# A four-layer fp32 trunk on one core: raw input transposed, its norm moved onto products, and a later order of heads

## The chip, the cores and the metric

The kernel runs on one core of one Trainium2 chip. What counts is the device time of one execution in microseconds (us). The engines are named as the profile names them: PE is TensorE (PEld its weight loads), DVE VectorE, ACT ScalarE, POOL GpSimd, SP SyncE, whose queue issues most DMAs. Each engine runs its own instructions strictly in program order.

## What is computed

A trunk of 256 tokens by 2048 channels with two mixers: a gated DeltaNet, an MLP, a sparse attention (DSA), an MLP, a final norm. The change touches the first mixer alone, apart from arguments.

```python
def rms_norm(x, g):
    y = xf * lax.rsqrt(jnp.mean(xf * xf, axis=-1, keepdims=True) + EPS)
    return y * g

def gated_deltanet(h, w_in, conv_w, a_log, dt_bias, out_norm, w_out):
    proj = h @ w_in                                  # h = rms_norm(x, norm_mix[0]); q, k, v, z, b, a
    qkv = silu(causal_conv(qkv, conv_w))             # 16 q/k heads, 32 v heads of 128
    q, k = l2norm(q) * 128 ** -0.5, l2norm(k)
    beta, g = sigmoid(b), -exp(a_log) * softplus(a + dt_bias)
    o = chunk_gated_delta_rule(q, k, v, g, beta)     # a triangular inverse in each chunk
    o = rms_norm(o, out_norm) * silu(z)
    return o @ w_out
...
h = h + gated_deltanet(rms_norm(h, norm_mix[0]), ...)
h = h + squared_relu_mlp(rms_norm(h, norm_mlp[0]), mlp_w_up[0], mlp_w_down[0])
```

## The kernel before

Every large product is made of three passes in a rounded fp32 format: each weight item of 128x1024 numbers is loaded as `raw`, copied by ACT to `whi`, and its rest made by DVE as `wlo` (class `Stream`, lines 131 to 173). `get` (line 144) hands out one item and keeps three items split ahead and four more loading. `mm3` (line 321) issues hi*hi, hi*lo and lo*hi. `by_channel` (line 359) and `by_token` (line 377) run such a product over their items. This is the **main stream** of PE; 24 of its matmuls with 256 columns, or 12 with 512, use up one item.

The opening (lines 402 to 470) loads `x` into `xin` in four quarters on the SP queue, then `ident` and eight rows of gains, squares `x`, makes the reciprocal root, scales `xin` in place (`normalise`) and transposes it block by block into `xT` (`first`). Weights are asked for behind those loads on the same queue.

The first mixer runs 16 groups `g` (lines 736 to 752), each with a `by_channel` of eight items for one q/k head and two v heads, an evacuation of its two PSUM banks into `s`, and a `by_token` of four items for the gate `z`. Small work runs beside it in generators: `delta(g)` (line 520) does the convolution and the masked products of one group; every second one goes on into `solved(p)` (line 598), which inverts the triangles of a pair of groups in four levels of 32x32 matmuls, joins them, applies them, normalises the result `o` (tile `Tt`) and transposes it into `hT`. Pair p holds heads 4p to 4p+3. Then the out-projection (line 758) takes its four column chunks: three of them early, without the last heads, then their late rest, then the fourth.

What sets the order is a planner at build time. `Pace` (line 28) keeps a modelled clock for each engine; after each k `bg.tick()` lets those generators advance whose modelled time has come. `ensure(key)` (line 345) is the other way in: where the main stream needs a result that isn't emitted yet, it calls `bg.step()` until it is, and each such step advances the **oldest** active generator (line 109), whichever one holds the key. What is emitted in this way stands on PE with no main matmul in between. The keys are `("v", g - 2)` before the evacuation of group g (line 739), since `s` has two buffers, and `("o", k)` for head k in the out-projection (line 388).

```python
    def ensure(key):
        while key not in ready:
            assert bg.step(), key
...
        chain = self.active[0] if due is None else min(self.active, key=lambda c: c[0])
```

In the rows of the order and the trace, `aux`, `acc` and `pk` are PSUM tiles; `aux<-Tc,yv` (after the change `aux<-Tc,Lc`) and `aux<-Lc,Tct` (`aux<-Pm,Tct`) are the two halves of a level, `aux<-r,Tt`, `aux<-yv,la` and `aux<-Tt,yv` the application of the inverse, `aux<-wide,Tt` the transposes of `o` by `ident`, `aux<-wide,s` those of v, and `acc<-xhi,whi`, `acc<-whi,xhi`, `acc<-whi,h` and their like the main stream.

Of the kernel before, what the change touches and what calls it, by code (L numbers as in the profile page):

```python
# [7 lines left out]
F32 = mybir.dt.float32  # L8
F32R = mybir.dt.float32r
I32 = mybir.dt.int32  # L10
AF = mybir.ActivationFunctionType
# [119 lines left out]
class Stream:  # L131
# [11 lines left out]

    def get(self):
# [3 lines left out]
        while self.split < min(i + ahead + 1, len(self.items)) or self.loaded < min(i + self.loads + 1, len(self.items)):  # L148
            while self.loaded < min(self.split + self.loads - self.ahead, len(self.items)):
                (n, w), pieces, _ = self.items[self.loaded]  # L150
                raw = self.raw_pool.tile([P, 1024], F32, name="raw")
                view = raw[:, : n * w].rearrange("p (n w) -> p n w", n=n)
                for at, src in pieces:
                    self.sync.dma_start(out=at(view), in_=src)
                self.raw[self.loaded] = raw
                self.loaded += 1
# [20 lines left out]
def tile_hybrid_trunk(ctx: ExitStack, tc: tile.TileContext, a: dict, out: bass.AP):  # L177
# [103 lines left out]
    add_mix_out(s_o, 16, 2)  # L281
# [114 lines left out]
    def early_chunks(tiles, key, nk, banks=()):  # L396

        outs = [by_token(nk // 2 - 2, h_part(tiles), key, outs=o) for o in (None, None, *banks)]
        return [by_token(2, h_part(tiles), key, outs=o, k0=nk - 4) for o in outs]


    with tc.tile_pool(name="first", bufs=1) as fp:
        xin = fp.tile([P, 2, D], F32, name="xin")
        rows = fp.tile([P, P], F32, name="rows")
# [5 lines left out]
        dve.memset(rows, 0.0)  # L410
        at = 0
        VEC = {}
        for name, src in (
# [7 lines left out]
        pool.dma_start(out=cwr, in_=a["dn_conv_w"][0].rearrange("t (c p) -> (t c) p", p=P).rearrange("(n q) p -> q n p", q=P))  # L421
# [694 lines left out]
```

## Time and profile before

| | us |
|---|---|
| median of three runs (lowest, highest) | 2590.46 (2588.62, 2592.14) |
| the profiled execution | 2591.25 |
| its span, first to last instruction | 2589.2 |
| PE busy in the span | 2545.4 |
| first matmul of the main stream | 18.28 |
| last group of the first mixer ends at about | 742 |

The engine with the most work is PE. A row of the timeline has its start, its duration, engine, operation, tiles (out<-in) and, in brackets, the idle time of the engine before it with what ended that. The idle time of an engine other than PE is of no concern by itself. All times below are of the profiled execution, from the start of its span.

### The profile page before, as it was taken

How to read it: one execution, taken by the hardware profiler on the slowest of the kernel's cores; microseconds unless marked ns; L12 is line 12 of the kernel's file. 1: busy time of each engine (PE TensorE's matmuls, PEld its weight loads, DVE VectorE, ACT ScalarE, POOL GpSimd, SP SyncE). 2: the span in 40 equal slices, each digit the busy share in tenths (PEclk: the TensorE clock that was granted, in tenths of full speed). 3: DMA queues.
4: the chain of work that ended last, by engine and by line, in shares of the span. 5: the costliest groups of instructions: out<-in, count | busy, mean ns of one | idle time of the engine just before them, and what ended most of it. 6: DMA issues, size and time to landing. Idle time of an engine off the chain costs nothing.

```text
span 2589.2 us, 52473 instructions
## 1 busy us (share of the span) xinstructions
PE 2545.4 (98%) x21827; PEld 2331.0 (90%) x21827; DVE 1534.8 (59%) x2179; ACT 1272.8 (49%) x1890; POOL 302.3 (12%) x512
## 2 busy tenths in 40 slices
PE   7999999999999999999999999999999999999998
PEld 7999999999977799988899988898899988999886
DVE  5867677668764655554455555576555544555544
ACT  5555555655544444443344444566544433444443
POOL 0434344334330000000000000000000000000000
PEclk9999999999999999999999999999999999999999
DMA  6655555555544566666666666644566666666664
GB/s 194 194 142 153 144 147 155 153 141 159 151 166 142 171 188 194 191 197 192 194 183 194 203 186 193 183 131 147 174 192 192 193 194 194 191 194 193 196 193 149
DMA packets 325966, 455.92 MB, mean 176 GB/s; under 512 B 18344, under 2 KB 159904, under 8 KB 325344
## 3 DMA queue, kind: packets, MB, share of 16 engines
q1 hardware_dynamic: 322320, 444.11, 57.1%
q10 hardware_dynamic: 3072, 7.11, 0.8%
q8 instruction: 171, 2.80, 0.4%
q0 software_dynamic: 336, 1.34, 0.1%
q14 instruction: 67, 0.55, 0.1%
HBM read 450.37 MB, written 2.13 MB: 175 GB/s over the span
## 4 chain that ended last, share of the span: by engine, by line
PE 90%; DVE 5%; ACT 2%; issue 1%; DMA 1%; POOL 0%; SPq 0%; ACTq 0%; DVEq 0%; POOLq 0%
PE acc L81 81%; PE aux L81 6%; PE pk L81 3%; DVE wlo L81 2%; DMA raw<-in_dn_w_in 1%; DVE Tct L81 1%; ACT Lc L81 1%; ACT whi L81 1%; DVE y L81 1%; DMA xin<-in_x 0%; DVE p L81 0%; DVE h L81 0%; DVE Tt L81 0%; DVE score L81 0%; ACT acc L81 0%
## 5 line engine op out<-in xcount | busy, mean ns | idle before, releaser
L81 DVE TENSOR_TENSOR wlo<-raw,whi 128x1024 fp32r<-128x1024 f32 x838 | 1026.1, 1233 | 860.7 <-ACT whi L81 857.4
L81 ACT CAST whi<-raw 128x1024 fp32r<-128x1024 f32 x838 | 874.4, 1049 | 852.4 <-PE acc L81 803.3
L81 PE MATMUL acc<-xhi,whi 128*128 128x256 f32 x3088 | 867.6, 281 | 0.3 <-ACT whi L81 0.3
L81 PE MATMUL acc<-xhi,wlo 128*128 128x256 f32 x3088 | 857.2, 278 | 1.2 <-DVE wlo L81 1.2
L81 PE MATMUL acc<-xlo,whi 128*128 128x256 f32 x3088 | 857.2, 278 | 0.9 <-issue 0.9
L81 PE MATMUL acc<-whi,h 128*128 128x512 f32 x2688 | 847.1, 392 | 4.0 <-ACT acc L81 2.0
L81 PEld LDWEIGHTS acc<-whi,h 128*128 128x128 f32 x2688 | 504.9, 188 | 111.0 <-ACT acc L81 2.9
L81 PEld LDWEIGHTS acc<-xhi,whi 128*128 128x128 f32 x3088 | 581.9, 188 | 3.0 <-ACT whi L81 0.7
L81 PEld LDWEIGHTS acc<-xlo,whi 128*128 128x128 f32 x3088 | 582.4, 189 | 1.2 <-issue 1.1
L81 PEld LDWEIGHTS acc<-xhi,wlo 128*128 128x128 f32 x3088 | 581.4, 188 | 1.7 <-DVE wlo L81 1.7
L81 PE MATMUL acc<-wlo,h 128*128 128x512 f32 x1344 | 524.9, 391 | 0.0
L81 PEld LDWEIGHTS acc<-wlo,h 128*128 128x128 f32 x1344 | 252.8, 188 | 49.9
L81 PE MATMUL acc<-whi,xhi 128*128 128x256 f32 (+2 forms) x576 | 171.7, 298 | 0.0
L81 PE MATMUL acc<-wlo,xhi 128*128 128x256 f32 (+2 forms) x576 | 166.3, 289 | 0.3 <-issue 0.3
L81 PE MATMUL acc<-whi,xlo 128*128 128x256 f32 (+2 forms) x576 | 166.4, 289 | 0.0
L81 POOL TENSOR_SCALAR E<-R,tokc 128x128 f32<-128x128 f32 x96 | 106.3, 1121 | 141.0 <-DVE y L81 89.6
L81 POOL DMA_DIRECT2D gain<-in_norm_final x1 | 0.6, 649 | 950.5 <-DVE nm L81 950.5
L81 PEld LDWEIGHTS acc<-whi,xhi 128*128 128x128 f32 x576 | 108.2, 188 | 2.6
L81 PEld LDWEIGHTS acc<-whi,xlo 128*128 128x128 f32 x576 | 108.4, 188 | 1.6 <-issue 0.4
L81 PEld LDWEIGHTS acc<-wlo,xhi 128*128 128x128 f32 x576 | 108.3, 188 | 1.3
L81 DVE SCALAR_TENSOR_TENSOR y<-s,cw,y 128x255 f32<-128x255 f32 (+2 forms) x192 | 93.4, 487 | 13.1 <-ACT y L81 8.5
L81 POOL TENSOR_TENSOR h<-h,gain 128x512 f32<-128x512 f32 x6 | 7.6, 1291 | 730.6 <-ACT acc L81 730.6
(257 smaller groups left out, 1942.5 us busy)
## 6 DMA issues: line engine op xcount, KB each, us to landing
raw<-in_mlp_w_up SPq DMA_DIRECT2D x256, 512.0 KB, 4.4
raw<-in_mlp_w_down SPq DMA_DIRECT2D x256, 512.0 KB, 4.2
raw<-in_dn_w_in SPq DMA_DIRECT2D x66, 512.0 KB, 4.0
raw<-in_dn_w_in SPq DMA_DIRECT2D x256, 128.0 KB, 2.6
raw<-in_dn_w_in SPq DMA_DIRECT2D x128, 256.0 KB, 3.3
raw<-in_dn_w_out SPq DMA_DIRECT2D x64, 512.0 KB, 3.7
raw<-in_dsa_w_out SPq DMA_DIRECT2D x32, 512.0 KB, 4.1
raw<-in_dsa_w_uq SPq DMA_DIRECT2D x16, 512.0 KB, 4.3
```

The source lines that it names most:

```text
L81: r = f(*args, **kwargs)
```

## The change

`x` is loaded in four blocks of 512 channels, the first on the SP queue and three on ACT's, behind the rows of the first gain and `ident`; the other gains go to POOL's queue, and the first weight items are asked for right behind the first block. The blocks are transposed without the norm. The norm is worked out after the transposes (`squares`, `rs0`) and applied later: as a row (`rs_row`, made by a matmul with ones) when the banks of q, k and v are evacuated, which DVE now does in place of ACT; as a scale of ACT's tanh for z; and by one more POOL multiplication in the output norm. PE gets 12 and 8 matmuls on ones ahead of and within the opening. The small products `ba` and `zo` of group 0 run before the evacuation of its banks. In the inverse, the four masked copies `Lm` by POOL are gone: each level multiplies the unmasked `Lc`, and DVE masks the product as it evacuates it, where ACT copied. The out-projection's first chunk stops at head 24, where the others stop at 28.

```diff
@@ class Stream
+    def fetch(self):
+        while self.loaded < min(self.split + self.loads - self.ahead, len(self.items)):
...
@@ streams of the out-projections
-    def add_mix_out(w, nk, n_early):
-        late = nk - 4
-        early = range(n_early)
-        for c, k0, k1 in [(c, 0, late) for c in early] + [(c, late, nk) for c in early] + [(c, 0, nk) for c in range(n_early, 4)]:
+    def add_mix_out(w, nk, late):
+        n_early = len(late)
+        for c, k0, k1 in [(c, 0, l) for c, l in enumerate(late)] + [(c, l, nk) for c, l in enumerate(late)] + [(c, 0, nk) for c in range(n_early, 4)]:
...
-    add_mix_out(w_o, 32, 3)
+    add_mix_out(w_o, 32, (24, 28, 28))
...
-    add_mix_out(s_o, 16, 2)
+    add_mix_out(s_o, 16, (12, 12))
@@ the opening
-        quarters = [(tb, slice(c * 1024, c * 1024 + 1024)) for c in range(2) for tb in range(2)]
-        for tb, s in quarters:
-            sync.dma_start(out=xin[:, tb, s], in_=a["x"][0, tb * P:tb * P + P, s])
-        sync.dma_start(out=ident, in_=a["consts"][:, 0:P])
+        warm_up(12)
+        act.dma_start(out=rows[0], in_=a["norm_mix"][0].rearrange("(n p) -> n p", p=P))
+        act.dma_start(out=ident, in_=a["consts"][:, 0:P])
+        for c in range(4):
+            (act if c else sync).dma_start(out=xin[:, :, c * 512:c * 512 + 512],
+                                           in_=a["x"][0].rearrange("(b p) d -> p b d", p=P)[:, :, c * 512:c * 512 + 512])
...
+        ws.fetch()
...
-            sync.dma_start(out=rows[at:at + n, :], in_=src.rearrange("(n p) -> n p", p=P))
+            if at:
+                pool.dma_start(out=rows[1][at - 16:at - 16 + n, :], in_=src.rearrange("(n p) -> n p", p=P))
...
-        rsqrt(rs, sq, 2)
...
-        def normalise(c):
+        def squares(c):
             s = slice(c * 512, c * 512 + 512)
-            act.activation(xin[:, 0, s], xin[:, 0, s], AF.Copy, scale=rs[:, 0:1])
-            dve.tensor_scalar(xin[:, 1, s], xin[:, 1, s], rs[:, 1:2], None, op0=OP.mult)
...
         def first():
             for k in range(KD):
...
-                if k % 4 == 1 and k < 12:
-                    normalise(k // 4 + 1)
-                yield
+                yield
+            for c in range(4):
+                squares(c)
+                yield
...
+            rsqrt(rs0, sq, 2)
+            dg = fp.tile([P, 2, P], F32, name="dg")
...
+            pe.matmul(t[:, :T], lhsT=ones, rhs=dg.rearrange("p b c -> p (b c)"), start=True, stop=True)
+            act.copy(rs_row, t[:, :T])
...
         bg.step()
         bg.step()
+        warm_up(8)
         first_banks = by_channel(8, x_part, "x0", ahead=3)
+        first_ba = by_channel(2, x_part, "x0", n_ct=1)[0]
+        first_zo = by_token(4, x_part, "x0", n_cols=256)
         bg.drain()
@@ solved
-            Pm, fold = Lc, yv.rearrange("p i b c -> p (i b c)")
-            Lm = fold.rearrange("p (n u c) -> p n u c", n=len(LEVELS), u=n_u)
+            fold = yv.rearrange("p i b c -> p (i b c)")
...
-            pool.tensor_tensor(Lm, Lc.unsqueeze(1).to_broadcast([P, n_l, n_u, B]),
-                               fine[:, 2:].unsqueeze(2).to_broadcast([P, n_l, n_u, B]), op=OP.mult)
-            yield True
+            yield
...
-                        pe.matmul(t[rows(q), u], lhsT=Lm[rows(q), n, u], rhs=Tc[rows(q), u], start=True, stop=True)
-                act.copy(Pm, t)
+                        pe.matmul(t[rows(q), u], lhsT=Lc[rows(q), u], rhs=Tc[rows(q), u], start=True, stop=True)
+
+                dve.tensor_tensor(Pm, t, each(fine[:, 2 + n]), op=OP.mult)
...
             pool.tensor_tensor(four(f), four(f), rep(sc), op=OP.mult)
+            pool.tensor_tensor(four(f), four(f), rs0.unsqueeze(1).unsqueeze(1).to_broadcast([P, 2, 2, 2]), op=OP.mult)
@@ the loop over groups
-                act.copy(s[:, 2 * c:2 * c + 2].rearrange("p n t -> p (n t)"), banks[c])
+                dve.tensor_tensor(s[:, 2 * c:2 * c + 2], banks[c].rearrange("p (n t) -> p n t", n=2),
+                                  rs_row.unsqueeze(1).to_broadcast([P, 2, T]), op=OP.mult)
             if g == 0:
-                bg.add(decays(by_channel(2, x_part, "x0", n_ct=1)[0]))
-            zo = by_token(4, x_part, "x0", n_cols=256)
+                bg.add(decays(first_ba))
+            zo = by_token(4, x_part, "x0", n_cols=256) if g else first_zo
...
-                act.activation(zg[:, b], zo[b], AF.Tanh, scale=0.5)
+                act.activation(zg[:, b], zo[b], AF.Tanh, scale=rs_half[:, b:b + 1])
...
-        chunks = early_chunks(hT, "o", 32, [[pkp.tile([P, 512], F32, name=f"pk{b}") for b in range(2)]])
+        chunks = early_chunks(hT, "o", 32, (24, 28, 28), [[pkp.tile([P, 512], F32, name=f"pk{b}") for b in range(2)]])
```

The edits also move the small work, since DVE's part in the planner's clocks grows. The order shows where.

PE around the end of `by_channel` in group 9 after the change: the two sets of transposes of pair 2, then steps of group 7, in one piece.

```order
L81 MATMUL acc<-xlo,whi 128x256
L81 MATMUL acc<-xhi,wlo 128x256
L81 MATMUL aux<-wide,Tt 128x128 x8
L81 MATMUL pk_6179<-s 128x512
L81 MATMUL pk_6180<-s 128x256
L81 MATMUL aux<-ones,y 128x1 x2
L81 MATMUL aux<-wide,s 128x128 x4
L81 MATMUL acc<-whi,xhi 128x256
```

Before, such a pair of transposes had main matmuls between its halves and was preceded by 132 to 156 of them since the last `aux<-yv,la`; here 72 precede it.

PE in the application of pair 3's inverse, before:

```order
L81 MATMUL aux<-Tt,yv 64x64 x8
L81 MATMUL acc<-xhi,whi 128x256
L81 MATMUL acc<-xlo,whi 128x256
L81 MATMUL acc<-xhi,wlo 128x256
...
L81 MATMUL aux<-r,Tt 128x128 x4
L81 MATMUL acc<-xhi,whi 128x256
L81 MATMUL acc<-xlo,whi 128x256
```

and after the change, at the end of `by_channel` in group 10, where `("v", 8)` is wanted:

```order
L81 MATMUL aux<-Tt,yv 64x64 x8
L81 MATMUL aux<-r,Tt 128x128 x4
L81 MATMUL aux<-yv,la_5432 128x128 x2
L81 MATMUL aux<-yv,la_6216 128x128 x2
L81 MATMUL aux<-r,Tt 128x128 x4
L81 MATMUL aux<-yv,la_5432 128x128 x2
...
L81 MATMUL aux<-yv,la_6217 128x128
L81 MATMUL aux<-wide,Tt 128x128 x8
L81 MATMUL acc<-whi,xhi 128x256
```

All that was spread between main matmuls, from the joining of the 32x32 blocks (`aux<-Tct,Pm`) to the transposes of `o`, stands there without one between.

PE at the out-projection, the transposes of pair 7, before (in the early part of the third chunk, `pk`) and after (in the late part of the first chunk, `acc`):

```order
L81 MATMUL pk_10903<-whi,h 128x512
L81 MATMUL pk_10903<-wlo,h 128x512
L81 MATMUL pk_10903<-whi,h 128x512
L81 MATMUL aux<-wide,Tt 128x128 x4
L81 MATMUL pk_10902<-whi,h 128x512
```

```order
L81 MATMUL acc<-wlo,h 128x512
L81 MATMUL acc<-whi,h 128x512 x2
L81 MATMUL acc<-wlo,h 128x512
L81 MATMUL acc<-whi,h 128x512
L81 MATMUL aux<-wide,Tt 128x128 x4
L81 MATMUL acc<-whi,h 128x512
```

Before, 60 main matmuls of 512 columns stood between pair 7's last `aux<-yv,la` and these transposes, after the change 36; for pair 6 it was 54, at the point where its first head was wanted, and is now 60, ahead of that point.

## Rows read from the trace of the kernel before

**Rows 1.** The page's first part: busy time, share of the span, instructions.

```profile
PE 2545.4 (98%) x21827; PEld 2331.0 (90%) x21827; DVE 1534.8 (59%) x2179; ACT 1272.8 (49%) x1890; POOL 302.3 (12%) x512
```

**Rows 2.** Busy time by stretch: us, engines (x instructions), granted clock, DMA share, GB/s.

```profile
584.00:673.00 89.00, 87.88 (x1279) 84.75 (x1278) 64.22 (x121) 50.95 (x99) 35.06 (x63) 1.00 0.54 149
960.00:1690.00 730.00, 730.00 (x4753) 664.40 (x4753) 390.58 (x408) 334.03 (x389) 0.00 (x0) 1.00 0.63 192
```

**Rows 3.** Timeline of the opening: the squares, the first cast, the first main matmuls.

```profile
5.34 1.06 ACT L81 ACTIVATE junk<-xin 128x1024 f32<-128x1024 f32 x1 [3.33 <-DMA xin<-in_x]
...
10.37 1.23 DVE L81 SCALAR_TENSOR_TENSOR junk<-xin 128x1024 f32<-128x1024 f32 x1 [2.55 <-DMA xin<-in_x]
...
17.19 1.99 ACT L81 CAST whi<-raw 128x1024 fp32r<-128x1024 f32 x2
...
18.28 0.58 PE L81 MATMUL acc<-xhi,whi 128*128 128x256 f32 x1 [0.28 <-ACT whi L81]
...
51.19 0.28 PE L81 MATMUL acc<-whi,xhi 128*128 128x256 f32 x1
```

**Rows 4.** The chain that ended last, a piece of it: start, us, what, how many.

```profile
43.17 13.01 PE acc L81 x115
```

**Rows 5.** PE's waits, from 0, 135 and 495 on: total, times, longest.

```profile
PE aux L81 <- DVE E L81: 1.5, 1, 1.5
...
PE aux L81 <- ACT Lc L81: 1.7, 1, 1.7
...
PE aux L81 <- DVE Tc L81: 2.2, 4, 0.7
```

**Rows 6.** PE's timeline where pair 6's result is wanted.

```profile
749.65 1.50 PE L81 MATMUL aux<-yv,la 128*128 128x128 f32 x12
...
763.62 1.03 PE L81 MATMUL aux<-wide,Tt 128*128 128x128 f32 x4 [0.22 <-DVE Tt L81]
765.42 0.50 PE L81 MATMUL acc<-whi,h 128*128 128x512 f32 x1 [0.78 <-ACT h L81]
...
767.16 0.74 PE L81 MATMUL acc<-whi,h 128*128 128x512 f32 x2 [1.00 <-DVE h L81]
```

**Rows 7.** Busy time by stretch in the opening; the bracket after PE counts matmuls.

```profile
5.00:6.00 1.00, 0.00 (x0) 0.00 (x0) 0.00 (x0) 0.66 (x1) 0.00 (x0) 1.00 1.03 422
...
20.00:22.00 2.00, 2.00 (x11) 2.00 (x11) 1.41 (x3) 0.00 (x0) 0.00 (x0) 1.00 0.65 149
22.00:24.00 2.00, 2.00 (x19) 2.00 (x18) 0.65 (x2) 1.61 (x3) 0.00 (x0) 1.00 0.86 228
```

**Rows 8.** Groups by shape, 584 to 673: xcount | busy, mean ns | idle before.

```profile
L81 POOL TENSOR_TENSOR yv<-Lc,fine 128x1024 f32<-128x1024 f32 x1 | 2.6, 2638 | 4.6 <-ACT Lc L81 4.6
...
L81 DVE TENSOR_TENSOR Tct<-Tct,fine 128x256 f32<-128x256 f32 x1 | 2.5, 2511 | 0.0
...
L81 DVE TENSOR_TENSOR Tc<-Tc,aux 128x256 f32<-128x256 f32 x4 | 1.7, 418 | 2.0 <-PE aux L81 2.0
```

**Rows 9.** Timeline of pair 7's chain on four engines, in order of time.

```profile
815.62 0.21 PE L81 MATMUL aux<-Lc,Tct 32*32 32x32 f32 x1
...
816.78 0.76 ACT L81 ACTIVATE Tt<-aux 32x256 f32<-32x256 f32 x2
...
826.70 1.05 PE L81 MATMUL aux<-yv,la 128*128 128x128 f32 x8
...
827.79 0.75 DVE L81 TENSOR_TENSOR r<-r,aux 128x256 f32<-128x256 f32 x2 [1.97 <-PE aux L81]
...
836.70 1.50 PE L81 MATMUL aux<-yv,la 128*128 128x128 f32 x12
...
848.92 1.22 POOL L81 TENSOR_TENSOR f<-f,sc 128x8 f32<-128x8 f32 x1
...
850.17 2.19 DVE L81 SCALAR_TENSOR_TENSOR Tt<-Tt,f,zg 128x128 f32<-128x128 f32 x8
```

**Rows 10.** Busy time by stretch behind PE's wait of 1.7 at 143.2; granted clock third from the end.

```profile
145.00:147.00 2.00, 2.00 (x11) 2.00 (x11) 1.93 (x5) 0.00 (x0) 2.00 (x3) 0.50 0.80 204
```

More of the change, by code (lines that the diff above doesn't have):

```diff
@@ L142, in add @@
         self.items.append((shape, pieces, turn))
+    def fetch(self):
+        while self.loaded < min(self.split + self.loads - self.ahead, len(self.items)):
+            (n, w), pieces, _ = self.items[self.loaded]
+            raw = self.raw_pool.tile([P, 1024], F32, name="raw")
+            view = raw[:, : n * w].rearrange("p (n w) -> p n w", n=n)
+            for at, src in pieces:
+                self.sync.dma_start(out=at(view), in_=src)
+            self.raw[self.loaded] = raw
+            self.loaded += 1
     def get(self):
@@ L148, in get @@
         while self.split < min(i + ahead + 1, len(self.items)) or self.loaded < min(i + self.loads + 1, len(self.items)):
[L149 to L156, printed above, removed]
+            self.fetch()
             if self.split >= min(i + ahead + 1, len(self.items)):
@@ L394, in by_token, with early_chunks @@
         return outs
-    def early_chunks(tiles, key, nk, banks=()):
-        outs = [by_token(nk // 2 - 2, h_part(tiles), key, outs=o) for o in (None, None, *banks)]
-        return [by_token(2, h_part(tiles), key, outs=o, k0=nk - 4) for o in outs]
+    def early_chunks(tiles, key, nk, late, banks=()):
+        outs = [by_token(l // 2, h_part(tiles), key, outs=o) for l, o in zip(late, (None, None, *banks))]
+        return [by_token((nk - l) // 2, h_part(tiles), key, outs=o, k0=l) for l, o in zip(late, outs)]
@@ L402, in tile_hybrid_trunk @@
+    carry = ExitStack()
+    carried = carry.enter_context(tc.tile_pool(name="carried", bufs=1))
+    tokc = carried.tile([P, 2, P], F32, name="tokc")
+    rs0 = carried.tile([P, 2], F32, name="rs0")
+    rs_half = carried.tile([P, 2], F32, name="rs_half")
+    rs_row = carried.tile([P, T], F32, name="rs_row")
     with tc.tile_pool(name="first", bufs=1) as fp:
         xin = fp.tile([P, 2, D], F32, name="xin")
-        rows = fp.tile([P, P], F32, name="rows")
+        rows = [fp.tile([n, P], F32, name=f"rows{n}") for n in (16, 56)]
@@ L405, in tile_hybrid_trunk, with warm_up @@
         cwr = fp.tile([P, 2, P], F32, name="cwr")
-        quarters = [(tb, slice(c * 1024, c * 1024 + 1024)) for c in range(2) for tb in range(2)]
-        for tb, s in quarters:
-            sync.dma_start(out=xin[:, tb, s], in_=a["x"][0, tb * P:tb * P + P, s])
-        sync.dma_start(out=ident, in_=a["consts"][:, 0:P])
-        dve.memset(rows, 0.0)
+        def warm_up(n):
+            warm = aux()
+            for _ in range(n):
+                pe.matmul(warm[:, 0:P], lhsT=ones, rhs=ones, start=True, stop=True)
@@ L411, in tile_hybrid_trunk, with vec @@
+        pool.dma_start(out=upper, in_=a["consts"][:, P:2 * P])
+        pool.dma_start(out=fine, in_=a["consts"][:, 2 * P:].rearrange("p (n c) -> p n c", c=B))
+        def vec(name, i=0):
+            return vecs[:, VEC[name] + i:VEC[name] + i + 1]
+        sq8 = fp.tile([P, 8], F32, name="sq8")
+        ws.fetch()
         at = 0
@@ L457, in first @@
                 ready.add(("x0", k))
-                if k % 4 == 1 and k < 12:
-                    normalise(k // 4 + 1)
                 yield
+            for c in range(4):
+                squares(c)
+                yield
+            sq = small_tile(2, "sq")
+            dve.tensor_reduce(sq, sq8.rearrange("p (b c) -> p b c", b=2), axis=AX.X, op=OP.add)
+            dve.tensor_scalar(sq, sq, 1.0 / D, EPS, op0=OP.mult, op1=OP.add)
+            rsqrt(rs0, sq, 2)
+            dg = fp.tile([P, 2, P], F32, name="dg")
+            for tb in range(2):
+                dve.tensor_scalar(dg[:, tb], ident, rs0[:, tb:tb + 1], None, op0=OP.mult)
+            yield
+            t = aux()
+            pe.matmul(t[:, :T], lhsT=ones, rhs=dg.rearrange("p b c -> p (b c)"), start=True, stop=True)
+            act.copy(rs_row, t[:, :T])
+            yield
             t = aux()
@@ L464, in first @@
             act.copy(cw, t[:, 0:T])
+            vectors(1, slice(16, 72))
         bg.add(first())
```

47 lines of the change are left out of this document (21 added, 26 removed).

## The prediction

> **What bounds the kernel now.** I read the page's first part, then busy time by stretch. PE is busy for 98% of the span [rows 1]; in an MLP stretch it is busy without a break, and in a steady pair of groups of the first mixer for 87.88 of 89.00 us, with DVE at 72% and ACT at 57% [rows 2]. So the span is the time of PE's main stream plus whatever PE waits. I then read the timeline of the opening and PE's waits. Three kinds of loss can be gained or added to by this change. First, the opening: the main stream starts at 18.28 and its first 27 us of work (eight items of q, k and v and two of `ba`, 240 matmuls at 0.113, as 115 of them in 13.01 us [rows 4]) end only at 51.19, where the first `z` matmul stands [rows 3]. Second, single waits in the first mixer [rows 5]. Third, places where a result is wanted before it is made: pair 6's, with 0.22, 0.78 and 1.00 us of idle time in a row [rows 6].
>
> **The opening.** Before, the four loads stand first on SP, the first quarter has landed at 5.34 and the last at 10.37; the squares, root and scaling follow, and transposes and casts until 18.28 [rows 3]. PE then runs at half speed at first: 11 matmuls in 20 to 22, 19 in the next 2 us [rows 7], which is 0.21 against 0.11 us each and costs some 1.7 us. After the change only the first block has to land. It shares the 16 engines with three more blocks, the first weights and POOL's loads; one queue alone already holds them at a share of 1.03 [rows 7], so a second queue adds no rate, and the block lands somewhat after the 5.34 of the first quarter: I take 6. The first weight item has 512 KB behind it and other blocks beside it; at 422 GB/s the 1 MB that may share with it takes 2.5 us more, so it is in place at 8.5 to 9, and a cast later (two take 1.99 [rows 3]), at 10, the stream starts. PE's 20 matmuls on ones fill time in which it waits, and let it start at full speed. The 27 us of stream and 24 transposes then end at 40.3, 10.9 earlier than the 51.19 of before. I take off 1.0 for the second item, whose pieces are issued late; 0.7 for the added matmul and transposes of the norm's row and gains; and 1.0 at the start of group 1, whose banks are those of group 0 and now wait for DVE. **Gain 8.2**, between 6 and 10.7.
>
> The Trainium skill says the same against two queues ("DMA: Bandwidth & Descriptors", section "Issuing engines are not separate DMA queues"): DMAs started by ACT, SP and POOL end on the same 16 engines and interleave. Had the second queue a rate of its own, the term would be 9.2 and not 8.2; no run here shows that yet.
>
> **Waits that go.** `decays` is emitted later against the stream, so that PE's 1.5 us on E goes [rows 5]: **gain 1.5**. In the inverse POOL's masked copies take 2.638 us, and DVE's small product beside them takes 2.511, where a product of the same shape takes 0.418 [rows 8]. Both go: the first operation, and some 2.1 us of the second. That delayed DVE step leads to PE's waits on Tc, 2.2 us in four for two pairs [rows 5], so 4.4 in the four pairs that look alike, and to longer ones in the first two pairs (1.7 on Lc with them [rows 5], 5.4 in all, and 1.6 of half clock behind one, below). Against that DVE gets, in two groups, four evacuations of 512 columns at some 0.75 (twice the 256 columns of `r`, 0.75 for two [rows 9]) and four masks at 0.418, together 4.7 us of 89, beside 2.1 gained: from 72 to 75%. ACT loses as many copies. That costs no time while the splits keep their lead of three items; without it each evacuation would delay PE by its 0.75. I take a **gain of 6.0** of 7.0 in the first two pairs and **3.0** of 4.4 later, since the transposes of o now stand 120 to 126 main matmuls (13.6 to 14.3 us) behind the last `aux<-yv,la`, not 132 (15.0), and may wait a little. The extra POOL operation in that chain (0.2 to 1.22, as its neighbour [rows 9]) lies in it.
>
> **Waits that come.** These decide. PE runs in order, so what stands in one piece in its order can't be hidden.
> A: at the end of group 9's products the transposes of pair 2 stand 72 matmuls, 8.2 us, behind its last `aux<-yv,la`. Pair 7's row shows how long the result takes: that matmul ends at 838.20 and scaling starts at 850.17, 12.0 later, and takes 2.19 [rows 9]; pair 6's is the same, 751.15 to the first transpose at 763.62 [rows 6]. So the first transposes wait some 4.6 and the last, behind the whole scaling, 5.5. Behind that ACT has two copies that wait for POOL's root of group 7 and 16 small ones that wait for DVE, before its next cast; the three items split ahead last 8.2 us, and I add 1.5. **Loss 7**, 5 to 9.
> B: at the end of group 10's products the whole application of pair 3 stands in one piece. Step by step from pair 7: six steps of a PE operation and its evacuation, of which the first takes 815.62 to 817.54 and the fourth 826.70 to 828.54 [rows 9], 1.7 to 1.9 each, are 10.8; two outputs at 1.4, 2.8; then to the scaling 12.0, in which some steps queue behind the main stream's splits, which stand still here (estimate 7 to 12); 0.3 for POOL's new operation; scaling 2.2; the last transposes 0.5. That is 24 to 29, of which 8.7 is PE's own work that is done elsewhere before. **Loss 17**, 15 to 20.
> C: at the out-projection pair 7 takes the place that pair 6 had, with 36 matmuls of 0.227, 8.2 us, in front. The first transposes wait 12.5 - 8.2 + 0.3 = 4.6, and the 2.0 of waiting on both halves' splits [rows 6] comes as before; pair 6's 2.2 go. **Loss 4.4**, 3 to 6.
> The clock: behind a wait of 1.7 us at 143.2 [rows 5] the granted clock was 0.50, that is 1.2 GHz, in 145 to 147 [rows 10], and 16 matmuls took 0.21: 1.6 us. A, B and C each hold a longer wait, and PE's own work in B would be slowed too: **loss 5**, 0 to 10. Beyond the first mixer nothing moves.
>
> **Sum.** Gains 8.2 + 1.5 + 6.0 + 3.0 = 18.7; losses 7 + 17 + 4.4 + 5 = 33.4; net 14.7 slower. The profiled execution took 2591.25 (its span and 2.05 around it), 0.8 above the median of the runs; on that median, 2590.46, the forecast is **2605**. With all gains at their upper ends and all losses at their lower ends it is 2592, the other way round 2624.
>
> **Rivals.**
> 1. *The wait at B hides.* For: much of its 24 us is ACT, DVE and POOL, which are idle then and could be faster than the rows. Against: even with 1.2 us for each of the six steps, and the shortest root, some 11 idle us remain. With this and the other gains at their best (23.7 against 5 + 11 + 3 and no half clock) the time is 2590.46 - 4.7, some 2586, no change; it needs all of it.
> 2. *Faster:* the opening is worth more than its first block. If the loads overlap so well that the stream starts at 7, right behind the transposes, it gains 3 more than the 8.2, and with rival 1's B and a full clock the time is about 2583. It decides if the stream starts before 8.
> 3. *The clock falls for long.* In B PE works some 9 of 25 us, in short pieces; at half speed these add 9, and A and C 2 each behind them: 2615 to 2620. For: rows 10 show it behind a shorter wait. Against: the single waits of 1 us at pair 6 did not show it.
> 4. *DVE becomes the bound.* In the order a pair's steps come 72 us of stream behind those of the pair before, where it was 65, as if DVE were too slow; if it is so in fact, splits come late by 1 us or so a group, 10 to 16 us in all: 2615 to 2620. Against: 75% of DVE.
>
> **How the numbers follow.** The forecast with its spread (2596 to 2614) has 0.62; rival 1 and other ways to end within 0.2% (B between 11 and 14 us of idle time, with the opening at its upper end), 0.17; rival 2, 0.07; rivals 3 and 4 together, 0.14. A measurement of this kernel can tell 0.2%, 5.2 us, from no change. Faster by more: 0.07; within: 0.18 (rival 1 and a hundredth of the forecast's lower edge); slower by more: 0.75. The range that leaves out 2 in 10, one above and one below, is 2588 to 2617.
>
> **What the profile will show.** The opening: the first main matmul near 10, at 0.11 from the start, and the first z matmul at 40 to 42; if it stands at 45 or later, the loads were the bound. The waits on E and Tc should be gone and the product beside POOL's masked copies be at 0.4. B: between pair 3's `aux<-Tct,Pm` and its transposes no main matmul and 24 to 29 us; A and C: 4 to 6 us of PE idle time ahead of the transposes; a granted clock of 0.50 behind each. The forecast is wrong if B is under 12 us of idle time, or if main matmuls in steady pairs wait on `wlo`.

## The result and the profile after

The changed kernel takes 2625.43 us (median of four runs, 2623.74 to 2628.34) against 2590.52: ratio 1.0134, 95% interval 1.0122 to 1.0147, 35 us slower. The forecast was 2605, slower, with a range up to 2617: the sign was right, the size was not, and the time lies above the range. The profiled execution, the slowest of the four, has a span of 2626.5 us where the one before had 2589.2, so the differences below add up to 37 and not to 35.

Since the main stream is the same in both, the times at which PE reaches the same point of it say where the time went:

| point of the main stream | before | after | difference |
|---|---|---|---|
| first matmul | 18.28 | 12.37 | -5.9 |
| first z matmul (group 0) | 51.19 | 47.77 | -3.4 |
| group 1, products begin | 62.07 | 60.47 | -1.6 |
| group 9, products begin | 408.45 | 394.92 | -13.5 |
| group 9, z begins | 434.88 | 431.39 | -3.5 |
| group 10, z begins | 484.11 | 509.11 | +25.0 |
| out-projection begins | 719.49 | 741.49 | +22.0 |
| end of the span | 2589.2 | 2626.5 | +37.3 |

A difference holds two things: waits and slow matmuls, and small work that stands earlier or later in the stream. To part them I took every PE instruction's time to the next one against the usual step of its form in the kernel before. This is an estimate, good to a us or two for each part. By it, 7.3 of the 11.9 us gained between group 1 and group 9 are small work that is only moved behind, and 4.7 are real. From group 9 on (A) 7.9 us are lost, in group 10 (B) 24.1, from the out-projection on (C) 11.7; group 11 to the out-projection gives 0.5. With the opening's 1.6 the losses less the gains are 36.9 of the 37.3.

The page's first part and PE's waits over the whole span (total, times, longest), after the change:

```profile
PE 2569.1 (98%) x21870; PEld 2349.1 (89%) x21870; DVE 1543.9 (59%) x2247; ACT 1250.9 (48%) x1828; POOL 279.7 (11%) x519
```

```profile
PE aux L81 <- DVE Tt L81: 15.1, 5, 7.4
PE aux L81 <- ACT y L81: 13.0, 7, 4.7
PE aux L81 <- DVE xlo L81: 2.0, 2, 1.4
...
PE aux L81 <- DVE Tc L81: 1.3, 1, 1.3
```

PE is as busy as in [rows 1] by share, and 24 us busier in sum, with 43 instructions more: part of that "busy" is half clock. The list has `Tt` (the transposes of `o`) and `y` at its head. "ACT y" is a near miss of the label: these seven waits all stand ahead of `aux<-Tc,Lc`, the first half of the inverse's first level, and what ends there is `Tc` on DVE, as the label says in other runs. So the waits on `Tc` of [rows 5] have not gone. With the one that keeps its label (1.3) they sum to 14.3 us. The kernel before had 6.0:

```profile
PE aux L81 <- DVE Tc L81: 6.0, 9, 1.6
```

B, PE's timeline in group 10 after the change (start, duration, idle time before):

```profile
480.12 0.60 PE L81 MATMUL aux<-wide,s 128*128 128x128 f32 x4
...
481.82 0.28 PE L81 MATMUL acc<-xhi,wlo 128*128 128x256 f32 x1
...
483.26 1.11 PE L81 MATMUL aux<-yv,la 64*64 64x64 f32 x16 [0.53 <-issue]
485.13 1.83 PE L81 MATMUL aux<-Tt,yv 64*64 64x64 f32 x16 [0.76 <-ACT yv L81]
487.64 2.08 PE L81 MATMUL aux<-r,Tt 128*128 128x128 f32 x8 [0.68 <-ACT Tt L81]
490.52 2.07 PE L81 MATMUL aux<-yv,la 128*128 128x128 f32 x8 [0.81 <-ACT yv L81]
493.11 2.08 PE L81 MATMUL aux<-r,Tt 128*128 128x128 f32 x8 [0.51 <-DVE r L81]
494.98 4.83 PE L81 MATMUL aux<-yv,la 128*128 128x128 f32 x24
507.17 2.29 PE L81 MATMUL aux<-wide,Tt 128*128 128x128 f32 x8 [7.37 <-DVE Tt L81]
509.11 0.56 PE L81 MATMUL acc<-whi,xhi 128*128 128x256 f32 x1
```

and busy time by stretch there (granted clock third from the end):

```profile
490.00:495.00 5.00, 3.96 (x17) 3.67 (x18) 1.06 (x5) 0.47 (x1) 0.00 (x0) 0.50 0.00 0
495.00:500.00 5.00, 4.80 (x25) 4.49 (x24) 0.00 (x0) 2.50 (x11) 0.00 (x0) 0.61 0.00 2
500.00:505.00 5.00, 0.00 (x0) 0.00 (x0) 0.68 (x4) 1.70 (x9) 1.70 (x9) 0.73 0.00 0
```

From the last main matmul at 481.82 to the next at 509.11 stand 27.3 us, as forecast (24 to 29). But the idle time in them is only 10.7 (0.53 + 0.76 + 0.68 + 0.81 + 0.51 + 7.37), not 15 to 20; the rest is PE's own work, stretched by a granted clock of 0.50: 24 of `aux<-yv,la` take 4.83 where 12 took 1.50 in [rows 9]. And the first row holds the point of the whole case: the wanted result, `aux<-wide,s` of group 8, is already in the stream, 1.7 us ahead of the piece. Only its key isn't set yet, and so the oldest generator, pair 3's, is stepped to its end.

A and C, PE's timeline:

```profile
426.03 2.22 PE L81 MATMUL aux<-wide,Tt 128*128 128x128 f32 x8 [3.11 <-DVE Tt L81]
...
442.68 1.08 PE L81 MATMUL aux<-Tc,Lc 32*32 32x32 f32 x64 [4.68 <-ACT y L81]
...
901.04 1.17 PE L81 MATMUL aux<-wide,Tt 128*128 128x128 f32 x4 [4.34 <-DVE Tt L81]
902.99 0.80 PE L81 MATMUL acc<-whi,h 128*128 128x512 f32 x1 [0.78 <-ACT h L81]
```

At A the transposes wait 3.11, less than the 5.5 forecast, but another 4.68 come at the next pair's first level, where the forecast had only 1.5, for late splits. At C the 4.34 is the forecast's 4.6.

The clock behind A's second wait and behind C, by stretch:

```profile
444.00:446.00 2.00, 2.00 (x11) 2.00 (x11) 1.93 (x4) 0.50 (x1) 2.00 (x3) 0.50 0.00 1
...
904.00:906.00 2.00, 2.00 (x6) 1.61 (x6) 0.00 (x0) 0.00 (x0) 0.00 (x0) 0.50 0.00 0
```

The opening, ACT's and PE's timeline and the stretch in which the clock is down:

```profile
11.28 1.04 ACT L81 CAST whi<-raw 128x1024 fp32r<-128x1024 f32 x1 [2.42 <-DMA raw<-in_dn_w_in]
12.37 0.39 PE L81 MATMUL acc<-xhi,whi 128*128 128x256 f32 x1 [0.89 <-ACT whi L81]
...
17.09 0.69 PE L81 MATMUL aux<-wide,xin 128*128 128x128 f32 x2 [1.43 <-DVE xlo L81]
```

```profile
16.00:18.00 2.00, 0.91 (x4) 0.91 (x5) 1.43 (x3) 0.30 (x2) 0.00 (x0) 0.50 1.10 309
18.00:20.00 2.00, 2.00 (x11) 2.00 (x11) 1.23 (x2) 2.00 (x3) 0.00 (x0) 0.50 1.00 271
```

The first weight item lands at 11.28, not at 8.5 to 9. The granted clock is 1.00 when the stream starts, and 0.50 from 14.2 to 21.

### The profile page after: what moved, and what is told of

Same layout as the page of the kernel before. It is cut to its first block, busy times and chain, and to the rows that moved or that the text cites. A ratio compares the mean times of both kernels' runs of the same rounds, so it can differ in the third digit from the quotient of the medians.

```text
span 2626.5 us, 52566 instructions
## 1 busy us (share of the span) xinstructions
PE 2569.1 (98%) x21870; PEld 2349.1 (89%) x21870; DVE 1543.9 (59%) x2247; ACT 1250.9 (48%) x1828; POOL 279.7 (11%) x519
## 4 chain that ended last, share of the span: by engine, by line
PE 74%; issue 3%; DVE 2%; ACT 2%; POOL 1%; ACTq 0%; POOLq 0%; DVEq 0%
PE acc L81 69%; PE aux L81 3%; PE pk L81 3%; POOL rs_u L81 1%; DVE wlo L81 1%; ACT Lc L81 0%; ACT whi L81 0%; POOL E L81 0%; DVE p L81 0%; DVE y L81 0%; POOL f L81 0%; DVE score L81 0%; ACT acc L81 0%; ACT h L81 0%; DVE h L81 0%
## 5 line engine op out<-in xcount | busy, mean ns | idle before, releaser
L81 POOL TENSOR_SCALAR E<-R,tokc 128x128 f32<-128x128 f32 x96 | 98.6, 1040 | 100.5 <-DVE wlo L81 83.5
```

The costliest lines, as they stand in the source:

```text
L81: r = f(*args, **kwargs)
```

## Experiments

Each time is a median in us; the ratio is to the kernel before as it was measured beside that run, with its 95% interval.

**What is forced, and what by.** Theory 1: the loss is made by results that are forced in one piece. Theory 2: DVE is too slow for the added work, and the forced places only show it.

`e1_force_earliest` advances, where a key is wanted, the generator that is due first:

```diff
         while key not in ready:
-            assert bg.step(), key
+            assert bg.step(float("inf")), key
```

> The changed kernel with one edit: where the main stream needs a result that is not emitted yet, the generator that is due first is advanced, not the oldest. In the order the transposes of pairs 2, 3 and 7 then have 12.2, 12.2 and 10.9 us of main matmuls between the last aux<-yv,la and themselves, where the changed kernel has 8.2, 0 and 8.2. Theory 1 (the loss is made by results forced in one piece, at the three places A, B and C, 43.7 us more idle and half-clock time there than before): A, B and C shrink to 2 to 3 us each, nothing else moves, 2582 to 2595 us. Theory 2 (DVE and its chain are too slow for the added work, and the forced places only show it): the waits come back in front of other steps and the time stays above 2610 us.

2617.71, ratio 1.0106 (1.0090 to 1.0121). A, B and C are gone as places (group 10's z begins 8.1 us earlier than before the change, where the changed kernel was 25.0 late), but 21.8 us are lost between there and the out-projection. The time lies in theory 2's range, and the waits did come back in front of another step; whether the reason is theory 2's, e9 tells. PE's waits from 400 to 740:

```profile
PE aux L81 <- DVE Tc L81: 20.4, 4, 5.1
```

and one of them on ACT, DVE and PE:

```profile
430.05 0.84 ACT L81 ACTIVATE r<-aux,nk 128x256 f32<-128x256 f32 x2 [3.90 <-POOL nk L81]
...
431.18 4.22 ACT L81 COPY Lc<-la 32x64 f32<-32x64 f32 x16
```

```profile
435.43 0.42 DVE L81 TENSOR_TENSOR Tct<-Lc,fine 128x256 f32<-128x256 f32 x1 [2.59 <-ACT Lc L81]
...
436.72 1.25 DVE L81 TENSOR_TENSOR s<-acc,rs_row 128x512 f32<-128x512 f32 x2
```

```profile
436.94 1.08 PE L81 MATMUL aux<-Tc,Lc 32*32 32x32 f32 x64 [5.11 <-DVE Tc L81]
```

The first level of the inverse waits for sixteen copies that ACT makes in 4.22 us, and DVE's evacuation of `s` stands behind them. Those copies are in the piece because `delta` sets its key only at the start of the step after the one that makes the result; for every second group that same step begins the inverse.

`e2_old_masks` is the changed kernel with the inverse of the kernel before (its POOL product, ACT copies and masks), all else as changed.

> The changed kernel with the inverse of the kernel before: POOL's masked copies and ACT's copies of the products are back, the masks on products are gone; the raw opening, the norm on products and the order of heads stay. In the order no result stands in one piece (13.6 us of main matmuls ahead of every pair's transposes). Theory 1 (forced pieces): the loss is gone, and what is left is the opening's own 1.6 us of gain and the waits on Tc as before: 2583 to 2592 us. Theory 2 (the evacuations that DVE now does, or the opening, make the loss): above 2605 us.

2596.07, ratio 1.0021 (1.0011 to 1.0030), between the two ranges and nearer to theory 1's: nothing forced, the loss gone but for 5 us. So the new masks are needed for the loss. PE's waits from 400 to 740 are longer than before, 11.6 us (6.0 of it on `Tc`, 1.5 in each of four) where they were 4.5; what makes them longer was not followed further than e10 below.

`e3_masks_only` is the kernel before with the new masks and nothing else.

> The kernel before with one part of the change: the inverse masks on products (no masked copies on POOL, DVE masks what ACT copied). In the order pair 6's application stands in one piece where its first head is wanted by the out-projection, 7 other pairs keep 12.9 us or more. Theory 1: the waits on Tc and Lc of the first two pairs go (3 to 5 us), one forced piece comes that costs what B costs in the changed kernel, 18 to 24 us, less the 2 us that pair 6 costs before: 2602 to 2612 us. Theory 2 (the masks only take work away, and a forced piece is cheap): 2580 to 2590 us.

2599.33, ratio 1.0035 (1.0021 to 1.0049): theory 1's one forced piece, at 2.7 us less than its range. The main stream reaches the out-projection 9.2 us earlier than before, and loses 17 there, at pair 6 in one piece. Its waits from 740 to 790:

```profile
PE aux L81 <- DVE Tt L81: 7.5, 1, 7.5
```

`e4_late_as_before` undoes the shorter first chunk in the changed kernel (`(24, 28, 28)` to `(28, 28, 28)`).

> The changed kernel with the first chunk of the out-projections stopping where it stopped before (28 and 12). In the order pair 6's application then stands in one piece ahead of head 24, and pair 7 has 13.6 us of main matmuls ahead of its transposes. Theory 1: C, 11.7 us more than before, goes, and a second piece like B comes, 18 to 24 us: 2632 to 2640 us. Theory 2 (the shorter first chunk itself is what costs at C): 2612 to 2618 us.

2632.30, ratio 1.0157 (1.0142 to 1.0172): C goes, and pair 6 stands in one piece with a wait of 7.8. The shorter chunk is worth 7 us in this kernel.

`e5_masks_and_heads` has both in the kernel before, and in the order nothing forced.

> The kernel before with two parts of the change: masks on products and the first chunk that stops at head 24 (12). In the order nothing stands in one piece: pair 6 has 13.6 us of main matmuls ahead of its transposes, pair 7 13.6. Theory 1 (the masks take waits away, and what costs is a result forced in one piece): the time of the masks alone, 2599.3, less its forced piece of some 16 us: 2581 to 2586 us, faster than the kernel before. Theory 2 (the shorter first chunk costs by itself, as the 11.7 us at C): 2592 to 2600 us.

2589.98, ratio 0.9994 (0.9985 to 1.0003), between the two ranges: no gain. PE is 8.3 us ahead at the out-projection and 0.9 at the end of the span: it owed small work and does it there. What theory 1 took for the masks' gain in e3 was mostly small work moved behind. From 400 to 740 waits on the first level have taken the place of the old ones (3.1 + 0.9 here, 4.5 on `Tc` before):

```profile
PE aux L81 <- ACT whi L81: 3.1, 3, 1.3
PE aux L81 <- DVE Tc L81: 0.9, 1, 0.9
```

In the order this is plain. The step with POOL's product was also a pause in the plan: 9.5 to 10.9 us of main matmuls stood between `aux<-wide,s` and the first level, and 6.1 to 8.2 are left.

`e6_planned_gap` puts 4 us of pause into the plan of e1 (`pace.chain += 4.0` ahead of the first level's `yield`).

> The kernel that advances the earliest generator (2617.7 us), with 4 us more planned between the sixteen copies into Lc and the first level of the inverse, so that 10.2 us of main matmuls stand between aux<-wide,s and that level, where there were 6.1 and before the change 9.5. No instruction is added. Pair 7's transposes get 6.8 us ahead of them instead of 10.9. Theory 1 (what is left there is PE's wait of 5.1 us for that first level in four pairs and the half clock behind it, because the step that POOL's masked copies took is gone from the plan): 25 to 30 us less and some 4 at the end more, 2588 to 2598 us. Theory 2 (DVE is late in fact, and a wait taken away comes back at the next step): above 2608 us.

2622.57, ratio 1.0119 (1.0104 to 1.0134). Theory 2's range came true; the waits are the splits' now:

```profile
PE acc L81 <- ACT whi L81: 9.6, 4, 2.4
PE acc L81 <- DVE wlo L81: 9.0, 4, 2.2
```

The sixteen copies and the evacuation still stand ahead of the next casts. A pause behind them can't help; they have to leave the forced piece.

`e9_key_a_step_earlier` does that, in the changed kernel, with one line moved:

```diff
                 act.activation(r[:, :, b], t[:, :, b], AF.Copy, scale=nk[:, b:b + 1])
-            yield
             ready.add(("v", g))
+            yield
             if j == 1:
```

> The changed kernel with one line of delta moved: the key (v, g) is set in the step that evacuates r, and not at the start of the next one, which for every second group also issues the sixteen copies into Lc and DVE's products on them. No instruction is added or taken away. In the order every pair then has 13.6 us or more of main matmuls ahead of its transposes, and the pairs come every 65.3 us of stream, where they came every 68 to 72. Theory 1 (what costs is that a wanted key drags more steps with it than it needs: at B the whole application, in the kernel that advances the earliest generator the sixteen copies ahead of the splits): A, B, C and the waits of 5.1 us go, 2588 to 2598 us. Theory 2 (the small work is late by itself, since in the order aux<-wide,s still stands at the end of the products from group 7 on): the waits of 5 us at the first level come in six pairs, 2610 us or more.

2591.66, ratio 1.0002 (0.9992 to 1.0012): 34 us come back, and A, B, C and the waits of 5.1 go. No instruction was added or taken away, so theory 2 is out for these 34 us. The kernel before sets its key at the same late place and steps the oldest generator too; neither is part of the change. The change moved the small work, as the order shows, to where a late key is felt.

Of its rows, the waits on `Tt` over the whole span (15.1 in the changed kernel), the waits from 400 to 740, and the clock behind two of these, which began at 429.9 and 520.6:

```profile
PE aux L81 <- DVE Tt L81: 0.2, 1, 0.2
```

```profile
PE aux L81 <- DVE Tc L81: 7.3, 4, 1.8
```

```profile
433.00:435.00 2.00, 2.00 (x19) 2.00 (x19) 1.93 (x4) 0.86 (x1) 0.00 (x0) 1.00 0.50 134
...
524.00:526.00 2.00, 2.00 (x11) 2.00 (x11) 1.96 (x4) 0.22 (x1) 0.00 (x0) 0.50 0.53 133
```

`e12_key_and_gap` adds a small pause to it, now that the copies can move (`pace.chain += 0.5` at the first level):

> The kernel with the key a step earlier (2591.7 us) and 0.5 us more planned ahead of the first level of the inverse: 7.5 us of main matmuls stand between aux<-wide,s and that level instead of 6.8; nothing else moves in the order. Theory 1 (what is left in the first mixer is PE's wait of 1.82 us for that level in five pairs, and granted clock 0.50 for some 4 us behind each, which costs as much again; waits of 1.1 us had no low clock behind them): each wait falls to 1.1, the clock stays up, 2.4 us a pair are gained: 2578 to 2584 us, faster than both kernels. Theory 2 (the wait moves to Pm or to a split, as it did in the kernel with a planned gap): 2588 us or more.

2584.63, ratio 0.9977 (0.9967 to 0.9986): faster than both kernels, 0.23% below the kernel before, and 0.6 us above what was expected of theory 1. One premise of that was wrong: of e9's five waits of 1.8, the clock fell to 0.50 for 3.4 us behind three (522, 615, 707) and stayed at 1.00 behind two (340, 432). Whether these 6 us are owed to the change or to the two edits of the plan isn't shown, since the kernel before was not run with those two alone. The waits of e12 and the same stretch:

```profile
PE aux L81 <- DVE Tc L81: 4.6, 4, 1.1
PE aux L81 <- DVE Pm L81: 1.0, 3, 0.6
```

```profile
523.00:525.00 2.00, 2.00 (x19) 1.93 (x18) 1.96 (x4) 1.47 (x2) 0.00 (x0) 1.00 0.52 133
```

**DVE's added work.** `e10_evacuation_on_dve` is the kernel before with `s` evacuated by DVE as a product with a row of ones.

> The kernel before with one part of the change by itself: the two banks of q, k and v are evacuated by DVE as a product with a row (here of ones), not copied by ACT. In the order nearly nothing else moves. Theory 1 (these evacuations stand in front of splits on DVE, which made a pair of groups 1 to 2 us longer in the kernel with the old masks than before): 2598 to 2606 us. Theory 2 (DVE has room, 72 to 75% busy, and the splits keep their lead): 2589 to 2593 us.

2593.06, ratio 1.0009 (0.9999 to 1.0019): 2 us, which the interval can't tell from none. The cover that the forecast named, the splits' lead, is there in this kernel.

`e15_evacuation_unplanned` is e9 with 1 us of pause, and the evacuation hidden from the planner's DVE clock.

> The kernel with the key a step earlier, 1 us more planned ahead of the first level (8.2 us of stream), and the evacuation of s not counted in the planner's DVE clock. Theory 1 (only the distance ahead of the first level matters): waits of 0.4 us in place of 1.8, no low clock: 2573 to 2580 us. Theory 2 (the evacuations are real, and what is planned without them comes late: waits on Pm of 1.2 to 2.8 us, as in the replanned kernel): 2586 us or more.

2586.28, ratio 0.9983 (0.9974 to 0.9992). The waits for the first level fall to 0.4, and others of 0.9 come on `Pm` behind it, with one of 2.75 at 253; 1.7 slower than e12, which their spread doesn't part. `e8_replanned` (all of the change with the key still late, evacuation hidden from the plan, 2 us of pause, loads as in e7, and group 0's decays ahead of its z) has more waits of this kind, though more than one of its edits can be the reason:

> All of the change, with four edits to its order alone: the loads in order of use, the decays of group 0 before its z and not behind it, the evacuation of s not counted in the planner's DVE clock, and 2 us more planned ahead of the first level of the inverse. In the order every pair has 13.6 us or more of main matmuls ahead of its transposes (the last one 10.9), and 8.2 to 10.2 us stand ahead of every first level. Theory 1 (the parts of the change are each worth something, and the loss is made by the plan): the opening's 5 to 8 us and some 5 us of waits are gained, 2574 to 2583 us. Theory 2 (DVE's added work delays the splits): 2592 us or more.

2612.00, ratio 1.0079 (1.0064 to 1.0094), with waits from 400 to 740 on a mask and on splits, as theory 2 said:

```profile
PE aux L81 <- DVE Pm L81: 6.7, 4, 1.8
PE acc L81 <- DVE wlo L81: 3.5, 3, 1.2
```

A part of its loss is the opening, where its z begins only at 55.35. `e11_masks_replanned` (e5 with the key a step earlier, 2 us of pause, and e1's edit) is a plan that I got wrong:

> The kernel before with the masks on products and the shorter first chunk (2590.0 us), and three edits to the plan: 2 us more ahead of the first level (9.5 us of stream instead of 6.8), the key (v, g) a step earlier, and the earliest generator advanced where a key is wanted. Theory 1 (its waits for the first level, 0.6 to 1.4 us in seven pairs, and the half clock behind some of them are what eats the masks' gain): 2580 to 2586 us. Theory 2 (they come back as late splits or late transposes, as in the kernel with a planned gap): 2588 to 2596 us.

2605.21, ratio 1.0055 (1.0039 to 1.0071), above both ranges: waits on `Pm` (5.3 from 400 to 740) and `Tc` (3.4) come back; which of its three edits brings them was not tried.

**The opening.** `e7_loads_in_turn` puts the changed kernel's first loads on SP in order of use:

```diff
+        def block(c):
+            sync.dma_start(out=xin[:, :, c * 512:c * 512 + 512],
...
         for c in range(4):
-            (act if c else sync).dma_start(out=xin[:, :, c * 512:c * 512 + 512],
...
+            block(c)
+            ws.fetch((1, 2, 4, 10 ** 6)[c])
```

The gains and constants stand behind them on the same queue.

> The changed kernel with its first loads in one queue in the order of use: block 0, first weight item, block 1, second item, block 2, two items, block 3, then the gains and constants. Nothing else moves. Theory 1 (the first weight item lands at 11.3 because the other blocks and the constants share the 16 engines with it): it lands at 7 to 8, the main stream starts at 8.5 to 9.5 instead of 12.4, the second item is there in time, the first z matmul stands at 42 to 44 instead of 47.8; 2619 to 2622 us. Theory 2 (the opening is bound by the transposes and their evacuation, or by the latency of a load): start not before 11.5, 2624 to 2627 us.

2628.71, ratio 1.0144 (1.0127 to 1.0160), above both ranges. The stream starts at 10.59, but the fifth weight item, which I had put behind the gains and constants, is late:

```profile
21.99 1.04 ACT L81 CAST whi<-raw 128x1024 fp32r<-128x1024 f32 x1 [4.93 <-DMA raw<-in_dn_w_in]
```

`e13_and_loads_in_turn` is e12 with that order but with gains and constants on POOL's queue as in the change, and `e14_and_no_warm_up` is e13 without the eight matmuls on ones.

> The kernel before this one in the list, with block 0, the first weight item, block 1, the second item, block 2, two items and block 3 on the SP queue in that order; the gains and constants stay on POOL's queue at the start. In the earlier try they stood on SP ahead of the fifth weight item, which landed at 22 us and held the stream for 6.1 us. Theory 1 (the opening is bound by what shares the 16 engines with the first items): main stream from 10.6 or earlier, no wait above 2 us behind it, first z matmul 2 to 4 us earlier than without the edit: 2 to 4 us faster. Theory 2 (the loads are bound by their sum, 5.6 MB in the first 20 us, whatever their order): first z matmul within 1 us, same time.

> As the one before, without the eight matmuls on ones within the opening (2 us at half clock). Theory 1 (they stand ahead of the first main matmul, which then waits for nothing else): the stream starts 1 to 2 us earlier and ends the opening as much earlier. Theory 2 (they fill time in which the stream waits for its weights, and keep the clock up): same start, and 1 to 3 us slower by matmuls at half clock.

2583.78 and 2584.87, ratios 0.9974 (0.9964 to 0.9984) and 0.9975 (0.9967 to 0.9984): no different from e12. The stream starts at 10.27 and 9.03 instead of 12.99, and the first z stands at 45.19 and 44.40 instead of 46.20. What is won at the start goes into waits for later blocks; in e13:

```profile
13.79 0.33 PE L81 MATMUL aux<-wide,xin 128*128 128x128 f32 x1 [1.91 <-DVE xlo L81]
```

```profile
24.38 0.33 PE L81 MATMUL aux<-wide,xin 128*128 128x128 f32 x1 [2.18 <-DVE xlo L81]
```

The stretch from 4 to 20 in the changed kernel, in e12 (the same opening) and in e13, where the last three columns are the granted clock, the DMA share and GB/s:

```profile
4.00:20.00 16.00, 10.38 (x63) 8.90 (x63) 5.44 (x8) 7.42 (x11) 3.81 (x8) 0.82 1.07 324
```

```profile
4.00:20.00 16.00, 11.87 (x76) 10.94 (x76) 5.89 (x9) 7.88 (x12) 3.82 (x8) 0.89 1.07 326
```

```profile
4.00:20.00 16.00, 13.28 (x102) 12.49 (x102) 7.88 (x12) 8.19 (x13) 3.81 (x8) 1.00 1.10 335
```

The 16 engines are full in all three, at nearly the same rate. The order of the loads moved the start by 2.7 us, the first z by 1.0 and the time not at all: theory 2, by which their sum sets the end. Without the matmuls on ones the first z comes 0.8 earlier and the time is 1.1 longer, which the runs can't part.

## Why the prediction was wrong

**What bounds the kernel, and the places.** Right. The main stream with PE's waits is the span; the loss is at A, B and C, where the order showed them, and the 27.3 us of B, the 0.50 clock behind each and the small product at 0.42 (it was 2.5 beside POOL's masked copies) came as the last part of the prediction said. Three sizes failed: both gains and the clock.

**Opening, 8.2.** This is the first step that failed. Measured were 3.4 at the first z and 1.6 at group 1 (1.6 to 3.5 over the eight kernels with this opening). The start came at 12.4 and not at 10, because the first weight item shared the engines longer than the 2.5 us that I worked out from 422 GB/s; the rate here was 324. The matmuls on ones let the stream start at a clock of 1.00, but behind its first waits it fell, and 20 matmuls at 0.21 cost some 2 more. Group 0's z took 12.7 where it took 10.9, for the norm's row, gains and a wait on `s`. e13 shows that even an earlier start is not worth its size: the 16 engines are full until 20 in either order. The prediction named that case itself ("if it stands at 45 or later, the loads were the bound") and did not let it into the range. The trace agrees with the rule of the Trainium skill that was weighed there ("DMA: Bandwidth & Descriptors", section "Issuing engines are not separate DMA queues"): with three queues the share is 1.07 and the rate 324 GB/s, not above what one queue had in [rows 7].

**Waits that go, 10.5 in all.** The second failure. Some 5 us came. E's 1.5 fell to 0.9. The old waits on `Tc` and `Lc` went, but a wait of 0.9 to 2.3 on `Tc` ahead of the first level took their place, in the steady pairs too, so that from group 11 to the out-projection 0.5 us is gained. The step that failed is "both go" of POOL's masked copies: I counted the operation and DVE's slow product, and not the pause that the operation was in the plan. The order had shown it: first level at 9.5 behind `aux<-wide,s` before, 6.1 to 6.8 after.

**A, B, C, 7 + 17 + 4.4.** As idle time A came as 7.8 and B as 10.7. C came as 5.9, which is 3.7 more than the 2.2 that pair 6 cost before. A is right as a sum and wrong in its parts: 3.1 at the transposes and 4.7 at the first level. B was put at 15 to 20 us of idle time and called wrong under 12; by that sign it was wrong, and only the length of the piece was right. Its six steps took 13.0 us and not 10.8, and the two outputs 4.8 and not 2.8, since PE worked at half clock in them. From there to the scaling it was 6.8, just below the estimated 7 to 12, since nothing queues beside that work (DVE waits 4.0 us for the root, whose POOL steps take 0.2 each there, where pair 7's row has 1.22); that the engines could be faster there than the rows, rival 1 had named. So the 27.3 us came out right by luck: less idle time than forecast, and slower work.

**The clock, 5.** The third failure, the largest on the side of the losses. It cost some 18 us: in B 7.8 within the piece and 1.6 behind it, at C some 3, at A 1.7 behind the first wait and 2.4 behind the second, and 1.6 behind a wait of 2.26 at 734. Rival 3 (the clock falls for long) had priced nearly this, at 9 within B and 2 behind each of the others, and put 2615 to 2620 on it; the reason against it, that single waits of 1 us at pair 6 had left the clock up, did not hold for waits of 3 to 7.

**The sum.** With measured sizes it is 6.8 gained, where 18.7 was forecast, against 22.2 of idle time and some 18 of half clock, where 28.4 and 5 were: some 33 slower, against a measured 35. The gains missed by 12 and the losses by 7, in the same direction. The prediction's own sum with all gains low and all losses high was 2624, a us and a half short of the result; its range stopped at 2617. (The sum at the other end, 2592, takes the waits' gains at 6.0 and 3.0, where rival 1 takes 7.0 and 4.4; with these it would be 2590.)

**What the forecast did not see.** Why there is a forced piece at all: one key, set a step too late, with the rule that the oldest generator is stepped. The prediction took the places for results "wanted before it is made". At B the result was there, 1.7 us ahead [the first row of B above]. With the key in its place the same change costs nothing (e9).

Rival 2 (faster, start before 8) did not come. Rival 4 (DVE the bound) did not either: e10 puts DVE's evacuations by themselves at 2 us, though with the rest of the change and the old masks (e2) 5 us are lost that no run here takes apart. Left open too is why e11's plan brings waits on `Pm` back, and how much of e9's remaining waits belongs to the later start of the small work.

## What to carry to other kernels

A step that is taken out of a chain takes its time out of the plan as well: look at what stood behind it and how far ahead its inputs are now. Where a scheduler forces a result "until the key is there", look at which statement sets the key and what else is issued until then; a key set one step late cost 34 us here, with the engines' work unchanged. And a wait is not to be priced by its idle time alone: at A, B and C PE's work within and behind the waits ran at half clock, which cost half as much again at A and C and nearly as much again at B.

## What the runs showed of the hardware

- The granted clock was 0.50 behind one wait of 1.8 us at the first level (e9, 524 to 526) and 1.00 behind a wait of 1.1 at the same place (e12, 523 to 525). But a wait of the same length did not always bring it down: it was 1.00 behind e9's equal wait at 432, and in the changed kernel two waits of 2.26 ahead of the same matmuls, which ended at 342.5 and 734.3, had these stretches behind them:

```profile
344.00:346.00 2.00, 2.00 (x19) 2.00 (x18) 1.93 (x4) 0.69 (x2) 0.00 (x0) 1.00 0.10 19
...
736.00:738.00 2.00, 2.00 (x12) 2.00 (x12) 1.93 (x5) 0.15 (x1) 0.00 (x0) 0.54 0.16 34
```

- Half a microsecond of pause in the plan (e12) took 0.7 us of wait off each of five pairs, and the low clock behind three of them, 7 us in all.
- The same opening ended at different times in different kernels, one profiled execution of each: the first z matmul stood at 45.97 (e9), 46.03 (e1), 46.20 (e12), 47.11 (e2) and 47.77 (the changed kernel), and the stretch of low clock lay at 9 to 13 in e1 and at 14 to 21 in the changed kernel. So the matmuls on ones did not hold the clock up in this opening.
- Sixteen copies of 32 partitions by 64 elements took ACT 4.22 us, 0.26 each; the planner counts 0.15.
